# Banded attention on one core: the values become the stationary operand, the result stays feature-major, and w_out's rows are reordered to match

## The chip, the core and the metric

The kernel runs as one program on one core of a Trainium2 chip. The core has a matrix engine (TensorE, written PE in the profile), a vector engine (DVE), a scalar engine (ACT), a general engine (POOL) and a queue processor (SP) that issues nearly all of the transfers. The metric is the device time of one execution in microseconds (us). Three runs of the kernel before gave 2034.96, 2035.17 and 2035.97 us; the median is 2035.17 us.

## The reference, cut to what matters

One layer of a decoder is computed for a prompt of 1024 tokens and for a sample group of 8 sequences with 8 new tokens each. All arithmetic is in float32.

```python
x = x + 0.5 * rms_norm(swiglu(rms_norm(x, norm_ffn1_pre), ...), norm_ffn1_post)
z = rms_norm(x, norm_mix_pre) @ w_in + b_in     # q, k, v and the four HGRN2 parts
# attention, 8 query heads on 2 key/value heads, window 128, one learned sink per head
s = einsum('bnqhgd,bnkhd->bnhgqk', q, k) * SCALE          # 128 queries by 256 keys, banded
p = exp(s - m) / (sum(exp(s - m)) + exp(sink - m))
a = einsum('bnhgqk,bnkhd->bnqhgd', p, v)                  # 512 features per token
a = rms_norm(a, attn_out_norm)                            # over the 512 features
# HGRN2: o, S = hgrn2_chunked(...), for the sample group from eight stored states
x = x + rms_norm(concat([a, o]) @ w_out, norm_mix_post)
x = x + 0.5 * rms_norm(swiglu(rms_norm(x, norm_ffn2_pre), ...), norm_ffn2_post)
```

The order in which the 512 attention features are held is free, as long as the rows of `w_out` and the gains `attn_out_norm` are held in the same order.

## The kernel before

The 1088 tokens are cut into three tiles, n = 0, 1, 2. Tile 0 has 320 tokens: two prompt blocks of 128 and the 64 sample tokens. Tiles 1 and 2 have three prompt blocks each. The two feed-forward layers (`make_ffn`) and the projections `w_in` and `w_out` make up most of the work. Each of their products is made of three float32r matmuls on two halves of each operand (`mm3`, L273 to L275), so that a weight tile is loaded by a transfer into one of three `raw` buffers, rounded on ACT (`split`, L252) and its remainder taken on DVE (L253).

The mixing (attention and HGRN2) runs as a stream of small steps beside these long matmuls. `mixer(n)` chains the attention blocks (`attn_block`) and, step by step in turn with them, the HGRN2 blocks (`hgrn_block`); each `yield` ends a step. `tick()` stands between the pieces of the long matmuls and lets each stream go forward by its rate; `need()` runs the rest of a stream at once. The program is then put through a scheduler (`schedule_with_timeline_sim=True`), which sets the final order of the instructions on each engine from its own model of their times. At run time every engine goes through its list strictly in that order.

An attention block has 128 queries. It is worked off in two passes (`pr`), each with two heads of each of the two key/value groups g. A pass has these steps: four score products (`sc`, L1099), whose operands lie in partitions 0 to 63 for g = 0 and 64 to 127 for g = 1; mask and maximum on DVE (L1107); the exponential on ACT (L1116); eight transposes of the probabilities on PE (`pT`, L1127) and their copy to SBUF on DVE (L1130); and the products with the values (`pv`, L1140). In the kernel before, the transposed probabilities (128 keys by 128 queries) are the stationary operand and 64 columns of the values move, once per head and key block: eight matmuls in a pass. The result has queries in partitions. After both passes DVE divides by the denominators (L1147), `finish_attn` takes the sum of squares on ACT (L1068), the inverse root on DVE in eight small operations (`rsqrt`), scales (L1071), transposes the four 128-wide parts back on PE (`oT`, L1075), applies the gains (L1077), and `put_mix` (L1062, L1063) writes the two halves into `MT`, the stationary or moving operand of the `w_out` products.

All small products are plain float32. The trace writes two matmuls and two weight loads for each such instruction, and one of each for a transpose. All of them share four PSUM banks (the tag `ax`); the long matmuls have four of their own (`mm`).

For the sample tokens, `sample_attn` has four rounds of products with cached and new values: L1326 (128 cached keys) and L1329 (8 new keys) in turn for four sequences, each sequence with 32 result partitions of its own. `sample_hgrn` has for each of four heads one product of L1365 (all 64 tokens) and eight of L1368, one per stored state: a stationary tile of 64 columns, in which the tokens of the other sequences are masked to zero (L1360, on POOL), against 128 moving columns.

`w_out` is loaded by one transfer per weight tile, eight tiles for each n.

## Time and profile before

| what | value |
|---|---|
| median of three runs | 2035.17 us |
| time of the profiled execution | 2035.28 us |
| span from its first to its last instruction | 2033.6 us |
| PE busy | 2002.3 us, 98% |
| DVE busy | 1445.4 us, 71% |
| ACT busy | 921.4 us, 45% |
| POOL busy | 550.4 us, 27% |
| the mixing steps | from 743 to about 1375 us |

A row of a group names the line, engine and operation, then out<-in by the program's names, the shapes, and xcount; behind the bar stand the busy time of the group in us, the mean length of one in ns, and the idle time of the engine just before them with what ended it. A shape such as `128*64 128x256` on PE means 128 rows by 64 columns of stationary operand and 256 moving columns. Matmuls overlap, so that the mean length of one is larger than its share of the time: the busy time of a group divided by its count is nearer to what it costs. In a timeline, a row has its start, its length until the last end, the line, the operation and the count of equal instructions merged; the distance of two starts is what the first one costs.

### The profile page before, as it was taken

Reading aid. Unit: us, or ns where it says so; the run is one execution under the profiler, and the core shown is the slowest. Engines: PE = TensorE matmul, PEld = TensorE weight load, DVE = VectorE, ACT = ScalarE, POOL = GpSimd, SP = SyncE. Lnnn points to the kernel's source line nnn. Section 1 sums busy time; section 2 is a strip of 40 time slices with the busy share of each in tenths; the row PEclk is TensorE's granted clock in tenths of the full one; section 3 lists DMA queues with packets and bytes.
Section 4 is the critical chain, followed back from the end, with each engine's and each line's share of the span. In section 5 each row is a group of like instructions: output and inputs, shape, how many; then the busy total and the mean of one; then the engine's idle time right before and its main releaser. Section 6 shows DMA issues by size and latency. Waiting matters only on the chain.

```text
span 2033.6 us, 34788 instructions
## 1 busy us (share of the span) xinstructions
PE 2002.3 (98%) x13337; PEld 1870.8 (92%) x13337; DVE 1445.4 (71%) x2429; ACT 921.4 (45%) x1647; POOL 550.4 (27%) x508
## 2 busy tenths in 40 slices
PE   9999999999999999899999999999999999999998
PEld 8999999999998988698899897998999999999886
DVE  5776667886568557877668856766889888655667
ACT  6534333444445435435343443644544444445452
POOL 0013333654104101311213311210146555510201
PEclk9999999999999999899999999999999999999999
DMA  8455445656777545546434243526565556576874
GB/s 253 143 158 164 146 143 164 205 179 217 234 240 215 169 147 180 166 127 182 133 96 146 83 142 94 172 95 208 158 203 195 199 175 202 207 236 223 287 258 136
DMA packets 371975, 360.09 MB, mean 177 GB/s; under 512 B 40194, under 2 KB 293969, under 8 KB 371793
## 3 DMA queue, kind: packets, MB, share of 16 engines
q1 hardware_dynamic: 371009, 356.42, 55.2%
q8 instruction: 105, 1.72, 0.4%
q10 hardware_dynamic: 800, 1.44, 0.2%
q14 instruction: 61, 0.50, 0.1%
HBM read 279.85 MB, written 78.94 MB: 176 GB/s over the span
## 4 chain that ended last, share of the span: by engine, by line
PE 94%; DVE 3%; DMA 2%; issue 1%; ACT 0%; DVEq 0%; SPq 0%; ACTq 0%
PE mm L273 27%; PE mm L274 27%; PE mm L275 27%; PE pv L1140 1%; PE c L275 1%; PE c L273 1%; PE c L274 1%; DMA raw<-in_ffn_w_gu_dram 1%; PE sc L1099 1%; PE lv L1171 1%; PE pT L1127 1%; PE tr L492 1%; DMA xt<-x1N 0%; PE l L1195 0%; PE sav L1368 0%
## 5 line engine op out<-in xcount | busy, mean ns | idle before, releaser
L273 PE MATMUL mm<-h,wsph 128*128 128x320 f32 (+1 forms) x1296 | 413.5, 321 | 3.5 <-DVE big L1451 3.1
L274 PE MATMUL mm<-h,wsph 128*128 128x320 f32 (+1 forms) x1296 | 412.1, 318 | 0.0
L275 PE MATMUL mm<-h,wspl 128*128 128x320 f32 (+1 forms) x1296 | 411.0, 318 | 0.0
L252 ACT CAST wsph<-raw 128x1024 fp32r<-128x1024 f32 x202 | 211.4, 1048 | 300.2 <-PE mm L274 240.2
L253 DVE TENSOR_TENSOR wspl<-raw,wsph 128x1024 fp32r<-128x1024 f32 x202 | 251.8, 1249 | 112.4 <-ACT wsph L252 112.0
L253 DVE TENSOR_TENSOR w<-raw,w 128x512 fp32r<-128x512 f32 (+1 forms) x226 | 248.0, 1101 | 92.1 <-ACT w L252 90.3
L252 ACT CAST w<-raw 128x512 fp32r<-128x512 f32 (+1 forms) x226 | 169.5, 754 | 209.8 <-PE mm L274 112.8
L273 PEld LDWEIGHTS mm<-h,wsph 128*128 128x128 f32 x1296 | 244.7, 189 | 8.3 <-DVE big L1451 3.5
L274 PEld LDWEIGHTS mm<-h,wsph 128*128 128x128 f32 x1296 | 245.1, 189 | 2.3 <-issue 1.0
L275 PEld LDWEIGHTS mm<-h,wspl 128*128 128x128 f32 x1296 | 244.7, 189 | 2.4 <-issue 1.8
L273 PE MATMUL mm<-h,w 128*128 128x384 f32 x704 | 235.6, 335 | 0.8 <-DVE big L720 0.8
L274 PE MATMUL mm<-h,w 128*128 128x384 f32 x704 | 235.6, 335 | 0.0
L275 PE MATMUL mm<-h,w 128*128 128x384 f32 x704 | 230.3, 335 | 0.0
L274 PE MATMUL mm<-w,h 128*128 128x512 f32 x462 | 181.0, 392 | 0.0
L273 PE MATMUL mm<-w,h 128*128 128x512 f32 x462 | 180.2, 393 | 0.0
L275 PE MATMUL mm<-w,h 128*128 128x512 f32 x462 | 179.7, 392 | 0.0
L275 PE MATMUL mm<-big,w 128*128 128x384 f32 x528 | 176.6, 335 | 1.2 <-DVE w L253 1.2
L704 POOL TENSOR_TENSOR big<-big 128x384 f32<-128x384 f32 x88 | 111.8, 1271 | 240.1 <-ACT big L717 121.2
L273 PE MATMUL mm<-big,w 128*128 128x384 f32 x528 | 176.6, 334 | 0.0
L274 PE MATMUL mm<-big,w 128*128 128x384 f32 x528 | 176.5, 334 | 0.0
L253 DVE TENSOR_TENSOR w<-t,w 128x512 fp32r<-128x512 f32 x176 | 161.0, 924 | 17.5 <-ACT w L252 17.3
L273 PEld LDWEIGHTS mm<-h,w 128*128 128x128 f32 x704 | 132.1, 188 | 1.3 <-DVE big L720 1.2
(349 smaller groups left out, 3874.1 us busy)
## 6 DMA issues: line engine op xcount, KB each, us to landing
raw<-in_ffn_w_gu_dram SPq DMA_DIRECT2D x156, 512.0 KB
raw<-in_ffn_w_down_dram SPq DMA_DIRECT2D x74, 512.0 KB
raw<-in_w_in_dram SPq DMA_DIRECT2D x54, 512.0 KB
ar<-fa SPq DMA_DIRECT2D x70, 384.0 KB
big<-in_ffn_w_down_dram SPq DMA_DIRECT2D x88, 256.0 KB
fb<-big SPq DMA_DIRECT2D x44, 512.0 KB
raw<-fb SPq DMA_DIRECT2D x40, 512.0 KB
fa<-big SPq DMA_DIRECT2D x22, 768.0 KB
```

The source lines that it names most:

```text
L252: S.copy(hi, src)
L253: (lo_eng or V).tensor_tensor(lo, src, hi.bitcast(F32), op=ALU.subtract)
L273: PE.matmul(out, a[0], b[0], start=first, stop=False, skip_group_check=resume)
L274: PE.matmul(out, a[0], b[1], start=False, stop=False, skip_group_check=resume)
L275: PE.matmul(out, a[1], b[0], start=False, stop=last, skip_group_check=resume)
L492: PE.transpose(bank[:, i * P:(i + 1) * P], y[kh][:, i, k * P:(k + 1) * P], ident)
L704: G.tensor_tensor(e[:, i], e[:, i], e[:, i + 1], op=ALU.mult)
L1099: PE.matmul(banks[g][:, i * 256:i * 256 + wk], zq[64 * g:64 * g + 64, 2 * pr + i, b * P:(b + 1) * P], kx[64 * g:64 * g + 64, k0:k0 + wk], ...
L1127: PE.transpose(bank[:, (i * nk + kb) * P:(i * nk + kb + 1) * P], pt[g][:, i, kb * P:(kb + 1) * P], ident)
L1140: PE.matmul(ob[:, hd * 64:hd * 64 + 64], pT[g][:, (i * nk + kb) * P:(i * nk + kb + 1) * P], vn[:, vb, g * 64:g * 64 + 64], start=kb == 0, ...
L1171: PE.matmul(b4[cs, a, :32], x[:, a, cs], y[:, a, cs], start=True, stop=True)
```

## The change

In `attn_block` the probabilities are divided by their denominator before they are transposed: DVE adds the sink's part and takes the reciprocal in each pass, then DVE scales the two heads of g = 0 and ACT the two of g = 1. The products with the values have the values as the stationary operand (128 keys by 64 features) and the transposed probabilities of two heads as 256 moving columns. The group g = 0 writes result partitions 0 to 63 and g = 1 partitions 64 to 127, in turn, so the result of a block has features in partitions: chunk m holds head m in its lower half and head 4 + m in its upper half. A pass has four such matmuls (two in the first block, which has one key block).

`finish_attn_t` takes the place of `finish_attn` for the prompt blocks. ACT squares the result from PSUM, PE sums over the features with four matmuls whose moving operand is one column of ones (`ms`, L1094), DVE takes the inverse root and puts it on a diagonal (L1098), one matmul with a stationary tile of ones spreads it over all partitions (L1100), ACT copies that to SBUF (L1102), and DVE multiplies result, gains and inverse root in four pieces (L1105). The transposes `oT` of the prompt blocks are gone; the sample tokens still go through `finish_attn`.

The gains and the rows of `w_out` are loaded in the new order: a `w_out` tile of the attention half comes with two transfers of 64 partitions, and for n = 0, where a tile holds both halves, with three instead of one. The sample products are split into 32-column pieces that alternate over result partitions.

```diff
             for pr in range(2):
...
+                V.tensor_tensor(of(mx[:, 2], pr), of(mx[:, 1], pr), of(sm[:, 2], pr), op=ALU.add)
+                V.reciprocal(of(mx[:, 3], pr), of(mx[:, 2], pr))
+                for g in range(2):
+                    for i in range(2):
+                        hd = 4 * g + 2 * pr + i
+                        t, r_ = pt[g][:, i, :wk], mx[:, 3, hd:hd + 1]
+                        if g:
+                            S.activation(t, t, AF.Copy, scale=r_)
+                        else:
+                            V.tensor_scalar(t, t, r_, None, op0=ALU.mult)
                 yield
...
-                for g in range(2):
-                    for i in range(2):
-                        hd = 4 * g + 2 * pr + i
-                        for kb in range(nk):
-                            vb = b + kb + (1 if first else 0)
-                            PE.matmul(ob[:, hd * 64:hd * 64 + 64],
-                                      pT[g][:, (i * nk + kb) * P:(i * nk + kb + 1) * P],
-                                      vn[:, vb, g * 64:g * 64 + 64], start=kb == 0, stop=kb == nk - 1)
-                yield
-            V.tensor_tensor(mx[:, 2], mx[:, 1], sm[:, 2], op=ALU.add)
-            V.reciprocal(mx[:, 3], mx[:, 2])
-            o = t2()
-            V.tensor_tensor(o.rearrange("p (h d) -> p h d", h=8), ob.rearrange("p (h d) -> p h d", h=8),
-                            mx[:, 3].unsqueeze(2).to_broadcast([P, 8, 64]), op=ALU.mult)
-            yield from finish_attn(n, o, P, slice(b * P, (b + 1) * P))
+                for kb in range(nk):
+                    vb = b + kb + (1 if first else 0)
+                    for g in range(2):
+                        PE.matmul(ob[64 * g:64 * g + 64, pr * 256:pr * 256 + 256],
+                                  vn[:, vb, g * 64:g * 64 + 64],
+                                  pT[g][:, :2 * wk].rearrange("p (i k t) -> p k i t", i=2, k=nk)[:, kb],
+                                  start=kb == 0, stop=kb == nk - 1, skip_group_check=True)
+                if pr == 0:
+                    yield
+            yield from finish_attn_t(n, ob, slice(b * P, (b + 1) * P))
...
+        def finish_attn_t(n, ob, sl):
+
+            sm, sq = small(), t2()
+            S.activation(sq, ob, AF.Square)
+            yield
+            bank = axbank("ms")
+            for m in range(4):
+                PE.matmul(bank[:, P:P + 1], sq[:, m * P:(m + 1) * P], ones[:, 0:1], start=m == 0, stop=m == 3)
+            V.tensor_scalar(sm[:, 0, 0:1], bank[:, P:P + 1], 1.0 / 512, EPS, op0=ALU.mult, op1=ALU.add)
+            rsqrt(sm[:, 1, 0:1], sm[:, 0, 0:1], (sm[:, 2, 0:1], sm[:, 3, 0:1]))
+            dg = sq[:, :P]
+            V.tensor_scalar(dg, ident, sm[:, 1, 0:1], None, op0=ALU.mult)
+            yield
+            PE.matmul(bank[:, :P], ones, dg, start=True, stop=True)
+            rb = sq[:, P:2 * P]
+            S.copy(rb, bank[:, :P])
+            o = t2((P, 4, P))
+            for m in range(4):
+                V.scalar_tensor_tensor(o[:, m], ob[:, m * P:(m + 1) * P], cols[:, C_AON + m:C_AON + m + 1], rb,
+                                       op0=ALU.mult, op1=ALU.mult)
+            put_mix(n, 0, sl, o)
+            yield
...
                     for i in range(4):
                         PE.matmul(ob[32 * i:32 * i + 32, :64], pT[:, 0, 32 * i:32 * i + 32],
-                                  vc[:, i, g * 64:g * 64 + 64], start=True, stop=False)
+                                  vc[:, i, g * 64:g * 64 + 64], start=True, stop=False, skip_group_check=True)
+                    for i in range(4):
                         c = i * P + g * 64
                         PE.matmul(ob[32 * i:32 * i + 32, :64], pT[:8, 1, 32 * i:32 * i + 32],
-                                  vnb[hb][:8, c:c + 64], start=False, stop=True)
+                                  vnb[hb][:8, c:c + 64], start=False, stop=True, skip_group_check=True)
...
-                PE.matmul(ob[:r, a * P:(a + 1) * P], At[:r, a, :r], z["v"][:r, 2, a * P:(a + 1) * P],
-                          start=True, stop=False)
-                for b in range(8):
-                    PE.matmul(ob[:r, a * P:(a + 1) * P], qm[:, b], st[:, b], start=False, stop=b == 7)
+                sr = [slice(32 * hf, 32 * hf + 32) for hf in range(2)]
+                for hf in range(2):
+                    PE.matmul(ob[sr[hf], a * P:(a + 1) * P], At[:r, a, sr[hf]], z["v"][:r, 2, a * P:(a + 1) * P],
+                              start=True, stop=False, skip_group_check=True)
+                for b in range(4):
+                    for hf in range(2):
+                        PE.matmul(ob[sr[hf], a * P:(a + 1) * P], qm[:, hf, b], st[:, 4 * hf + b], start=False,
+                                  stop=b == 3, skip_group_check=True)
...
+        def w_out_rows(k0, k1, c0, c1):
+
+            if k0 >= 4:
+                return [((ALL, slice(k0, k1) if c1 - c0 == P else ALL), w_out[k0 * P:k1 * P, c0:c1].rearrange(
+                    "(k p) m -> p k m", p=P))]
+            return [((slice(64 * g, 64 * g + 64), slice(k0, k1) if c1 - c0 == P else ALL),
+                     w_out[256 * g + 64 * k0:256 * g + 64 * k1, c0:c1].rearrange("(k p) m -> p k m", p=64))
+                    for g in range(2)]
...
-                    wt = load_up(w_out, d * P)
+                    wt = load_w(w_out_rows(0, 4, d * P, d * P + P) + w_out_rows(4, 8, d * P, d * P + P), pp, "wsp", 8)
```

The scheduler sets the order anew, so the change also moves instructions that the diff doesn't touch. Three places on PE show it; in their rows the size is that of the result (partitions by columns), the numbers tell buffers apart, and the line numbers are those of each kernel (L278 to L280 after are L273 to L275 before, L1204 is L1171, L1165 is L1127, L1228 is L1195, L1277 is L1244 and L454 is L449).

The first is the end of the second attention block of tile 0, around 847 us. `lv` and `l` are levels of HGRN2, `tr` and `kT` are transposes of other streams. Before:

```order
L275 MATMUL mm_8255<-w_8375,h_8433 128x512
L1171 MATMUL lv_8285<-t_1112_7909,t_1113_7910 32x32 x16
L1140 MATMUL pv_8007<-vn_6437,t_1159_8243 128x64 x4
L1140 MATMUL pv_8007<-vn_6437,t_1161_8250 128x64 x4
L1195 MATMUL l_1178_8352<-t_1112_7909,t_1113_7910 32x32 x8
L1195 MATMUL l_1186_8418<-t_1112_7909,t_1113_7910 64x64 x4
L1075 MATMUL oT_8456<-ident,t_1184_8404 128x128 x4
L449 MATMUL tr_8469<-ident,big_5758 128x128 x3
L449 MATMUL tr_8475<-ident,big_5758 128x128 x3
L1244 MATMUL kT_8481<-ident,t_1113_7910 128x128 x4
L449 MATMUL tr_8488<-ident,big_5758 128x128 x3
L273 MATMUL mm_8650<-h_8465,wsph_8646 128x384
```

After:

```order
L280 MATMUL mm_8274<-w_8393,h_8450 128x512
L1204 MATMUL lv_8217<-t_1112_7926,t_1113_7927 32x32 x16
L1165 MATMUL pT_8257<-ident,t_1139_8106 128x128 x4
L1165 MATMUL pT_8264<-ident,t_1140_8109 128x128 x4
L1204 MATMUL lv_8304<-t_1112_7926,t_1113_7927 32x32 x16
L1176 MATMUL pv_8024<-t_1159_8262,vn_6438 64x256
L1176 MATMUL pv_8024<-t_1161_8269,vn_6438 64x256
L1176 MATMUL pv_8024<-t_1159_8262,vn_6438 64x256
L1176 MATMUL pv_8024<-t_1161_8269,vn_6438 64x256
L1228 MATMUL l_1180_8370<-t_1112_7926,t_1113_7927 32x32 x8
L1094 MATMUL ms_8420<-ones,t_1173_8333 128x1 x4
L1228 MATMUL l_1187_8435<-t_1112_7926,t_1113_7927 64x64 x4
```

The wait for the transposes `oT` has left the list there (the spreading product comes 21 rows behind `ms`), but the transposes `pT` and one more `lv` now stand in the same run without a long matmul between them; before, eleven long matmuls stood between those and the rest.

The second is a pass of the second block of tile 1, where the products with the values stand among long matmuls. Before:

```order
L274 MATMUL mm_11100<-h_9245,wsph_11096 128x384
L1171 MATMUL lv_11028<-t_1537_10662,t_1538_10663 32x32 x16
L1140 MATMUL pv_10777<-vn_8641,t_1583_11000 128x64 x4
L1140 MATMUL pv_10777<-vn_8641,t_1585_11007 128x64 x4
L275 MATMUL mm_11100<-h_9243,wspl_11097 128x384
```

After:

```order
L278 MATMUL mm_11222<-h_9261,wsph_11218 128x384
L1176 MATMUL pv_10826<-t_1583_11051,vn_8658 64x256
L279 MATMUL mm_11222<-h_9263,wsph_11218 128x384
L1176 MATMUL pv_10826<-t_1585_11058,vn_8658 64x256
L1176 MATMUL pv_10826<-t_1583_11051,vn_8658 64x256
L1176 MATMUL pv_10826<-t_1585_11058,vn_8658 64x256
L280 MATMUL mm_11222<-h_9261,wspl_11219 128x384
```

The first product of g = 0 stands alone, and a long matmul separates it from the other three. Of the 16 passes, five have all four products in one run, two (the first block) have their two in one run, and nine are cut into one and three like this one.

The third is a round of the sample attention. Before:

```order
L1326 MATMUL spv_8717<-kv_8583,t_1233_8666 32x64
L1329 MATMUL spv_8717<-vnew_8525,t_1233_8666 32x64
L1326 MATMUL spv_8717<-kv_8583,t_1233_8666 32x64
L1329 MATMUL spv_8717<-vnew_8525,t_1233_8666 32x64
L1326 MATMUL spv_8717<-kv_8583,t_1233_8666 32x64
L1329 MATMUL spv_8717<-vnew_8525,t_1233_8666 32x64
L1326 MATMUL spv_8717<-kv_8583,t_1233_8666 32x64
L1329 MATMUL spv_8717<-vnew_8525,t_1233_8666 32x64
```

After:

```order
L1259 MATMUL hT_8699<-ident,t_1225_8639 128x128 x4
L1359 MATMUL spv_8734<-kv_8600,t_1233_8683 32x64 x4
L1363 MATMUL spv_8734<-vnew_8542,t_1233_8683 32x64 x4
L1204 MATMUL ld_8771<-big_6780,big_6644 32x32 x8
L1334 MATMUL ssc_8803<-big_8546,t_1213_8564 32x136 x4
```

The four products with cached values now follow each other, and so do the four with new values, each set over four different groups of 32 result partitions.

34 lines of the change are left out of this document (18 added, 16 removed).

## The prediction

> **What bounds the kernel now.** I read the page's shares and chain first, then two stretches of the mixing.
>
> ```profile
> span 2033.6 us, 34788 instructions
> PE 2002.3 (98%) x13337; PEld 1870.8 (92%) x13337; DVE 1445.4 (71%) x2429; ACT 921.4 (45%) x1647; POOL 550.4 (27%) x508
> PE 94%; DVE 3%; DMA 2%; issue 1%; ACT 0%; DVEq 0%; SPq 0%; ACTq 0%
> ```
>
> ```profile
> 743.00:1375.00 632.00, 618.30 (x5245) 545.48 (x5245) 452.61 (x1083) 287.32 (x591) 128.06 (x182) 0.99 0.46 136
> 843.00:865.00 22.00, 13.31 (x149) 11.73 (x150) 19.67 (x54) 12.35 (x28) 6.32 (x8) 0.77 0.64 163
> ```
>
> PE is busy for 98% of the span and is 94% of the chain. In the mixing it is idle for 632.0 - 618.3 = 13.7 us, of which 22.0 - 13.31 = 8.7 us lie between 843 and 865, where DVE is busy for 19.67 of 22 us. So the time of the change is PE's time for the altered products, plus what it does to waits, chiefly in that stretch. The sum is made against the profiled execution, 2035.28 us (1.7 around the span); the median of the runs, 2035.17, is 0.1 lower. The next rows are PE's groups.
>
> ```profile
> L1140 PE MATMUL pv<-vn,t 128*128 128x64 f32 x240 | 29.8, 274 | 0.1
> L1127 PE MATMUL pT<-ident,t 128*128 128x128 f32 x120 | 16.9, 277 | 0.0
> L1075 PE MATMUL oT<-ident,t 128*128 128x128 f32 x32 | 5.3, 292 | 3.5 <-DVE t L1071 3.5
> L1171 PE MATMUL lv<-t,t 128*32 128x32 f32 x1328 | 19.9, 199 | 2.4 <-DVE sm L1144 1.2 <-DVE sm L390 0.7 <-DVE t L1206 0.2
> L1195 PE MATMUL l<-t,t 128*32 128x32 f32 x128 | 4.7, 198 | 0.9 <-DVE t L1206 0.9
> L324 PE MATMUL st<-omean,ss 128*128 128x1 f32 x20 | 2.5, 229 | 0.0
> L336 PE MATMUL rb<-dg,ones 128*128 128x320 f32 x10 | 3.6, 442 | 0.0
> ```
>
> Of two equal shapes, `lv` goes round four column strips and costs 19.9/1328 = 15 ns a record; `l` stays in one strip and costs 4.7/128 = 37 ns. So column strips do overlap here, by a factor of 2.5 over four. For wider products the timeline of PE shows single runs among long matmuls, from several places:
>
> ```profile
> 1014.92 0.31 PE L275 MATMUL mm<-h,wspl 128*128 128x320 f32 x1
> 1015.07 1.89 PE L1140 MATMUL pv<-vn,t 128*128 128x64 f32 x16
> ...
> 1017.00 0.31 PE L274 MATMUL mm<-h,wsph 128*128 128x320 f32 x1
> 1017.15 0.31 PE L275 MATMUL mm<-h,wspl 128*128 128x320 f32 x1
> ...
> 1020.80 0.31 PE L275 MATMUL mm<-h,wspl 128*128 128x320 f32 x1
> 1021.04 1.14 PE L1099 MATMUL sc<-kx,big 64*128 64x256 f32 x8
> 1022.11 0.41 PE L273 MATMUL mm<-h,wsph 128*128 128x320 f32 x1
> 1022.36 0.31 PE L274 MATMUL mm<-h,wsph 128*128 128x320 f32 x1
> ...
> 1053.41 0.34 PE L275 MATMUL mm<-h,wspl 128*128 128x384 f32 x1
> 1053.68 1.13 PE L1099 MATMUL sc<-kx,big 64*128 64x256 f32 x4
> ...
> 1055.02 0.34 PE L274 MATMUL mm<-h,wsph 128*128 128x384 f32 x1
> 1055.20 0.34 PE L275 MATMUL mm<-h,wspl 128*128 128x384 f32 x1
> ```
>
> I call the cost of a run the distance from the long matmul before it to the second one behind it, less two ordinary steps (0.15 us each at 320 columns, 0.18 at 384). `pv`, 16 records: 1017.00 - 1014.92 - 0.29 = 1.79, or 0.112 a record. `sc` going between the two groups, 8 records: 1.56 - 0.29 = 1.27. `sc` of one group alone, 4 records: 1.61 - 0.35 = 1.26. Eight records in two strips cost what four cost in one: two strips overlap fully, at 1.07/4 = 0.267 us a record and strip, and entering and leaving such a run costs about 0.2 together (0.24 and 0.25 where an ordinary step is 0.15).
>
> **The change, part by part.**
>
> *Products with the values.* Before: 240 records at 0.112 = 26.9 us. After, 60 instructions, 120 records of 256 moving columns. One record costs at most `sc`'s 0.267, and half of its weight columns are gone; a full load is about 0.11 (`pv`'s record is no shorter), so half a load saves up to 0.055: 0.21 to 0.267, I take 0.24. The order decides how many overlap: five passes in one run, 4 x 0.24 + 0.2 = 1.16 each; nine cut, where the lone product costs 2 x 0.24 + 0.2 = 0.68 and the other three again 1.16 (two of the three share a strip); two short ones of the first block, 0.68 each. That is 5.8 + 16.6 + 1.4 = 23.8: 3.1 us less. Bounds: with 0.21 and no loss from the cuts 15.8 (-11); with no overlap at all 120 x 0.267 + 25 x 0.2 = 37 (+10). Only the Trainium skill speaks against the strips: "TensorE: Matmul & The Clock Gate", Part 3, says that a weight load overlaps matmuls in flight only if its row group differs. Column strips share their rows, so by that rule each of the 120 loads (about 53 ns, an estimate from the page's load formula for 64 columns) would stand in line, and the sum would be some 3 us higher. The 15 ns of `lv`, less than the 27 ns that the same formula gives for its load alone, disagree with it; I don't count it.
>
> *End of a block.* Added on PE for eight blocks: `ms`, 64 records with a full load and one column, 0.112 (load, as `pv`) to 0.125 (`st`, 2.5/20): 7.2 to 8.0; `L1100`, 16 records, by `rb` 0.36 x 128/320 = 0.144: 2.3. Removed: 32 transposes, 0.112 (a full load) to 0.165 (their row): 3.6 to 5.3. Net +4.2 to +6.7; I take +5, as the load was the price in `pv`. The DVE rows that go:
>
> ```profile
> L1147 DVE TENSOR_TENSOR t<-pv,sm 128x512 f32<-128x512 f32 x8 | 5.5, 684 | 4.0 <-PE pv L1140 4.0
> L1071 DVE TENSOR_SCALAR t<-t,sm 128x512 f32<-128x512 f32 x8 | 4.2, 526 | 0.2
> L1077 DVE TENSOR_TENSOR t<-oT,cols 128x512 f32<-128x512 f32 x8 | 5.5, 689 | 3.5 <-PE oT L1075 3.2
> L1116 ACT ACTIVATE t<-t,sm 128x256 f32<-128x256 f32 (+1 forms) x64 | 30.9, 485 | 37.9 <-DVE sm L1112 30.5 <-DVE sm L1118 7.4
> ```
>
> That is 1.9 us a block on DVE; it gets four scalings of 256 columns (half of L1071's, 1.1 us), four multiplications of 128 (a quarter of L1077's or a bit more, 0.7 to 1.4), a diagonal and four small ones: about as much, up to +1.5 a block, under PE in a stage where DVE is busy for 72%. ACT gets four scalings as long as its exponentials, 2 us a block, and is busy for 45%. Both cost nothing while PE has long matmuls.
>
> *Scores.* Their products stay, but the order puts them into two runs of one group in eight of the 16 passes where it was seven: 2 x 1.26 - 1.27 = +1.25, from 0 to +2.5; I take +1.
>
> *Sample products.* The run of HGRN2's stored states and a round of the attention products:
>
> ```profile
> 953.24 0.30 PE L1326 MATMUL spv<-kv,t 128*32 128x64 f32 x2
> ...
> 955.05 0.87 PE L449 MATMUL tr<-ident,big 128*128 128x128 f32 x6
> ...
> 983.85 0.44 PE L273 MATMUL mm<-h,wsph 128*128 128x384 f32 x1
> 984.23 1.96 PE L1368 MATMUL sav<-big,t 128*64 128x128 f32 x16
> ...
> 986.40 0.34 PE L275 MATMUL mm<-h,wspl 128*128 128x384 f32 x1
> ```
>
> `sav` costs 2.55 - 0.35 = 2.20 for 16 records, 0.125 each without 0.2. In two strips by turns: 8 x 0.125 + 0.2 = 1.2, a gain of 1.0 for each of four heads, less 0.2 for each of three cuts: -3.4 (0 without overlap, -4.5 without cuts). L1365's product becomes two halves side by side: nothing. The POOL mask of half the size hides under PE. `spv` costs 955.05 - 953.24 = 1.81 and 0.2 a round. After: 16 records of twice `l`'s moving width, 2 x 37/2.5 = 30 ns, 0.5 us, and 0.3 for two sets; 1.2 us less in each of four rounds: -4.8 (-3 to -6).
>
> *Transfers.* 16 more issues for n = 0 and 8 for n = 1 and 2, none with more bytes. SP needs 0.37 us for one, and no wait of PE in the mixing names a transfer; the weights are asked for well ahead. Nothing, +3 if a split load lands late. The extra transfer of gains lies in the first feed-forward stage: nothing.
>
> ```profile
> 971.79 0.37 SPq L259 DMA_DIRECT2D raw<-in_w_out_dram  x1
> ```
>
> *Waits.* The long gap of PE:
>
> ```profile
> 846.87 0.39 PE L275 MATMUL mm<-w,h 128*128 128x512 f32 x1
> ...
> 855.23 1.08 PE L1195 MATMUL l<-t,t 128*64 128x64 f32 x8 [3.22 <-DVE t L1206]
> ...
> 859.78 1.09 PE L1075 MATMUL oT<-ident,t 128*128 128x128 f32 x4 [3.46 <-DVE t L1071]
> ...
> 863.26 0.42 PE L273 MATMUL mm<-h,wsph 128*128 128x384 f32 x1
> ```
>
> For 16 us PE does only small pieces, and DVE's list sets the pace. The 3.46 us before `oT` go, for the spreading product stands 21 rows later; what is late next is the transposes `tr` and the rounded tiles behind them, which wait for the same DVE list, now with the scaling at its head. I take -2, from -6 to +4. Elsewhere the transposes `pT` now wait for one more step: two small DVE operations, two scalings of 0.26 on DVE and two of 0.49 on ACT beside them, about 1.3 us; behind them on both engines stand the weight roundings. Before, `pT` never waited (its row: 0.0), so most of it hides; +0.5, at worst 16 x 1.3 = +21.
>
> Sum: -3.1 + 5 + 1 - 3.4 - 4.8 - 1.5 = -6.8, so 2035.28 - 6.8 = 2028.5 us.
>
> **Rivals.**
> *The strips do better.* For it: `sc` overlaps fully; against it: nine cut passes. Values at -8 instead of -3.1, the gap at -5 instead of -2: 2021, and 2016 at the ends of both.
> *The longer way to the transposes takes the gain back.* For it: ACT's scaling queues behind roundings, and several passes have few long matmuls between scores and transposes. Against it: the idle 0.0. At 0.3 to 0.6 us a pass it costs 5 to 10: 2033 to 2038, no change. From 0.7 us a pass, 2040 and slower.
> *Wide column streams don't overlap.* Only 32-wide ones are seen to, and `sc`'s strips are strips of rows. Then values cost +10 and `sav` gains nothing: 13 + 3.4 more than forecast, 2045. It decides once a record in two strips costs over 0.21 us instead of 0.12, which makes up the 11 us to the upper edge of no change. Against it: `lv`.
>
> **How the numbers follow.** What a measurement tells from no change is about 0.2%, 4 us. Forecast (2023 to 2031): 0.46. Strips better: 0.18. Gain taken back to within 4 us: 0.21. Slower by the longer way: 0.08; by streams that don't overlap: 0.07. So faster 0.64, same 0.21, slower 0.15. From 2016 to 2040 all but the slower cases and the far end of the first rival are in.
>
> **What would show it.** `pv` at 0.12 us a record in whole runs and 0.24 where it stands alone; `ms` near 0.11; `sav` and `spv` at half their busy time; `oT` only four records; PE's idle time in the mixing no longer than 14 us; idle before `pT` near 0. The prediction is wrong if `pv` keeps over 0.2 us a record in its whole runs, or if `pT`, `ms` or L1100 show waits of over 5 us together.

## The result and the profile after

Six runs of the changed kernel took 2045.63 to 2051.17 us, median 2049.18; the six runs of the kernel before beside them have a median of 2035.07. The ratio is 1.0066, with a 95% interval of 1.0053 to 1.0079: the change costs 14 us where a gain of 7 was forecast. The profiled execution took 2047.08 us, 11.8 more than that of before. First the page of the changed kernel, span and busy time.

```profile
span 2045.3 us, 34828 instructions
PE 2006.7 (98%) x13273; PEld 1856.7 (91%) x13273; DVE 1452.6 (71%) x2493; ACT 933.5 (46%) x1679; POOL 550.1 (27%) x508
```

Span less PE's busy time is 38.6 us, before it was 31.3: idle time has grown although PE's list has 64 records fewer. PE is also busy for 4.4 us more.

Both traces have 10294 records of long matmuls, so the same record can be looked up in each. The 4300th starts 0.3 us earlier after than before, the 6800th 11.3 us later, and at the end it is 11.7. The whole loss lies in the mixing. The windows below run from the 4300th to the 6900th long matmul (stretch; then PE, weight loads, DVE, ACT, POOL; then the granted clock of TensorE), and under each stand the parts of it in which the trace has the granted clock at half. Before:

```profile
738.35:1412.14 673.79, 657.06 (x5469) 577.60 (x5468) 477.76 (x1136) 305.29 (x626) 128.06 (x182) 0.99 0.46 138
852.99:863.23 10.24, 4.53 (x25) 4.41 (x26) 8.16 (x22) 3.02 (x8) 2.08 (x4) 0.50 0.42 102
1266.01:1272.83 6.82, 6.04 (x23) 6.04 (x24) 5.18 (x27) 2.17 (x9) 0.00 (x0) 0.50 0.12 35
```

After:

```profile
738.02:1423.41 685.39, 663.30 (x5405) 565.01 (x5404) 484.24 (x1200) 317.44 (x658) 129.58 (x182) 0.97 0.46 136
847.40:867.88 20.48, 14.52 (x97) 10.88 (x98) 15.89 (x47) 9.61 (x22) 4.42 (x8) 0.50 0.52 136
1239.94:1243.34 3.40, 3.14 (x7) 2.49 (x8) 2.69 (x8) 3.07 (x13) 0.80 (x2) 0.50 0.00 0
1267.24:1274.06 6.82, 5.33 (x16) 4.42 (x17) 6.41 (x29) 2.63 (x14) 0.00 (x0) 0.50 0.28 83
1355.99:1362.81 6.82, 6.05 (x51) 4.57 (x52) 4.69 (x10) 3.38 (x5) 0.66 (x1) 0.50 0.39 103
```

The stretch is 11.6 us longer. PE is idle for 685.39 - 663.30 = 22.1 us in it, before for 16.7: +5.4. At half clock it works for 14.52 + 3.14 + 5.33 + 6.05 = 29.0 us, before for 10.6; if work at half clock takes twice as long, 14.5 us are lost, before 5.3: +9.2. What is left, length less idle less that loss, is PE's own work at full clock: 685.4 - 22.1 - 14.5 = 648.8, before 651.8: -3.0. So the work did get less, and waits and clock took back nearly five times as much. Set against the sum of the prediction, PE's work is 2.3 us above its forecast (-3.0 for -5.3), the waits are 6.9 above theirs (+5.4 for -1.5), and 9.2 belong by this reckoning to the clock, for which the sum has no term.

By place, between the same long matmuls, the changed kernel gains 2.7 us up to the 5100th (974 us: the crowd of small pieces near 850 us and the sample products, which alone gain 7.8 there), loses 1.8 from there to the 6200th (1230 us), and loses 12.5 from there to the 6900th, in the mixing of tile 2. Of these 12.5 us, 6.0 are idle time, 4.2 the loss at half clock and 2.2 work.

The two longest waits of PE after, by who ended them:

```profile
PE pT L1165 <- DVE t L1158: 4.4, 2, 2.5
PE mm L278 <- DVE big L1496: 2.6, 3, 1.5
```

At the head stands the wait of the transposes for the scaled probabilities (L1158), which did not exist before. 1.9 us of it lie near 848 us, 2.5 us in the last block. PE in the last block, from the scores to the next long matmuls:

```profile
1346.91 1.14 PE L1127 MATMUL sc<-kx,big 64*128 64x256 f32 x8
...
1353.77 0.46 PE L1204 MATMUL lv<-t,t 128*32 128x32 f32 x32 [0.68 <-DVE sm L1146]
1356.76 1.54 PE L1165 MATMUL pT<-ident,t 128*128 128x128 f32 x6 [2.53 <-DVE t L1158]
1358.23 0.66 PE L1204 MATMUL lv<-t,t 128*32 128x32 f32 x32
...
1361.19 0.47 PE L280 MATMUL mm<-h,wspl 128*128 128x320 f32 x1
1361.45 0.47 PE L278 MATMUL mm<-h,wsph 128*128 128x320 f32 x1
```

After the waits of 0.68 and 2.53 us, long matmuls that take 0.147 us a step elsewhere take 0.26 (1361.19 to 1361.45), until the clock is back at 1362.8. What PE waited for stands on ACT and DVE:

```profile
1355.71 0.19 ACT L1147 ACTIVATE sm<-sm 128x4 f32<-128x4 f32 x1
1355.81 1.03 ACT L255 CAST wsph<-raw 128x1024 fp32r<-128x1024 f32 x1
1356.74 0.91 ACT L1156 ACTIVATE t<-t,sm 128x256 f32<-128x256 f32 x2
```

```profile
1355.94 0.17 DVE L1149 TENSOR_TENSOR sm<-sm,sm 128x4 f32<-128x4 f32 x1 [0.52 <-ACT sm L1147]
1356.13 0.18 DVE L1150 RECIPROCAL sm<-sm 128x4 f32<-128x4 f32 x1
1356.35 0.62 DVE L1158 TENSOR_SCALAR t<-t,sm 128x256 f32<-128x256 f32 x2
```

From the end of the last exponential (1355.90) to the scaled tile of g = 0 (1356.97) it is 1.1 us; g = 1 stands behind a weight rounding of 1.03 us on ACT and comes at 1357.65. The scaling also has to wait for all four exponentials and for the sink's, because the denominators of all four heads are added in one operation (L1149), while the transposes of g = 0 need only the first two exponentials, which end at 1354.73. So the new step keeps PE from these transposes for 2.0 us, until 1356.76.

Near 848 us the way is much longer, though the operations are the same:

```profile
840.00 0.19 ACT L1147 ACTIVATE sm<-sm 128x4 f32<-128x4 f32 x1
```

```profile
842.40 0.75 DVE L426 SCALAR_TENSOR_TENSOR big<-big,sm,xt 128x512 f32<-128x512 f32 x1 [4.35 <-DMA xt<-in_x_prompt_dram]
...
846.06 0.15 DVE L1149 TENSOR_TENSOR sm<-sm,sm 128x4 f32<-128x4 f32 x1
846.91 1.20 DVE L426 SCALAR_TENSOR_TENSOR big<-big,sm,xt 128x512 f32<-128x512 f32 x1 [0.69 <-DMA xt<-in_x_prompt_dram]
...
848.24 0.62 DVE L1158 TENSOR_SCALAR t<-t,sm 128x256 f32<-128x256 f32 x2
```

The last exponential ends at 840.2 us and the scaled tile comes at 848.85, 8.7 us later: on DVE's list the four operations stand between additions of the residual (L426), which wait for transfers of `xt`. In eight of the sixteen passes this way takes 1.06 or 1.07 us, in seven 0.9 to 3.6. Before, DVE waited for `xt` there too, 4.24 us, but the transposes did not depend on it.

Before, the pass of the last block had its transposes 7.5 us behind its scores with no wait:

```profile
1339.86 1.13 PE L1099 MATMUL sc<-kx,big 64*128 64x256 f32 x4
...
1347.36 1.09 PE L1127 MATMUL pT<-ident,t 128*128 128x128 f32 x8
```

In its order 36 long matmuls stand between the two; after, 29 do, for a longer way. This count alone does not tell which passes wait: in the changed kernel the pass near 1128 us has 26 and does not wait, and the one near 848 us has 42 and waits 1.9 us. The groups of PE that changed:

```profile
L1176 PE MATMUL pv<-t,vn 128*64 128x256 f32 x120 | 24.8, 418 | 1.1 <-DVE t L1168 1.1
L1094 PE MATMUL ms<-ones,t 128*128 128x1 f32 x64 | 8.5, 254 | 0.0
L1406 PE MATMUL sav<-big,t 128*32 128x128 f32 x64 | 5.3, 277 | 0.0
L1100 PE MATMUL ms<-t,ones 128*128 128x128 f32 x16 | 3.4, 293 | 0.0
L1359 PE MATMUL spv<-kv,t 128*32 128x64 f32 x32 | 1.3, 231 | 0.0
L1363 PE MATMUL spv<-vnew,t 8*32 8x64 f32 x32 | 1.3, 226 | 0.0
```

`pv` has 24.8 us instead of 29.8, `sav` 5.3 instead of 8.3, the two `spv` groups together 2.25 instead of 7.53 (before, their rows overlap in time, so that the busy times of the two groups, 4.8 and 4.7, must not be added); `oT` keeps 4 of its 36 records.

### The profile page after: what moved, and what is told of

Its sections match the earlier page's. It is cut to its first block, busy times and chain, and to the rows that moved or that the text cites. A ratio compares the mean times of both kernels' runs of the same rounds, so it can differ in the third digit from the quotient of the medians.

```text
span 2045.3 us, 34828 instructions
## 1 busy us (share of the span) xinstructions
PE 2006.7 (98%) x13273; PEld 1856.7 (91%) x13273; DVE 1452.6 (71%) x2493; ACT 933.5 (46%) x1679; POOL 550.1 (27%) x508
## 4 chain that ended last, share of the span: by engine, by line
PE 91%; DVE 3%; DMA 3%; ACT 1%; issue 1%; SPq 0%; DVEq 0%; ACTq 0%
PE mm L278 27%; PE mm L279 26%; PE mm L280 26%; PE c L280 1%; PE c L278 1%; PE c L279 1%; PE sc L1127 1%; DMA ar<-fa 1%; PE pv L1176 1%; DMA raw<-in_ffn_w_gu_dram 1%; PE lv L1204 1%; PE pT L1165 1%; PE tr L497 1%; DVE w L256 1%; DMA xt<-in_x_prompt_dram 0%
## 5 line engine op out<-in xcount | busy, mean ns | idle before, releaser
L278 PE MATMUL mm<-h,wsph 128*128 128x320 f32 (+1 forms) x1296 | 414.7, 322 | 3.7 <-ACT sg L632 2.2
L280 PE MATMUL mm<-h,wspl 128*128 128x320 f32 (+1 forms) x1296 | 411.7, 318 | 0.0
L278 PEld LDWEIGHTS mm<-h,wsph 128*128 128x128 f32 x1296 | 244.6, 189 | 11.0 <-issue 3.1
L280 PEld LDWEIGHTS mm<-h,wspl 128*128 128x128 f32 x1296 | 244.7, 189 | 4.0 <-issue 3.5
L278 PE MATMUL mm<-h,w 128*128 128x384 f32 x704 | 235.8, 335 | 1.2 <-DVE big L725 1.2
L280 PE MATMUL mm<-h,w 128*128 128x384 f32 x704 | 230.5, 335 | 0.0
L278 PE MATMUL mm<-w,h 128*128 128x512 f32 x462 | 180.8, 395 | 0.5 <-DVE big L905 0.5
L280 PE MATMUL mm<-w,h 128*128 128x512 f32 x462 | 179.5, 392 | 0.0
L280 PE MATMUL mm<-big,w 128*128 128x384 f32 x528 | 176.8, 335 | 1.5 <-DVE w L256 1.5
L278 PE MATMUL mm<-big,w 128*128 128x384 f32 x528 | 176.6, 335 | 0.0
L278 PEld LDWEIGHTS mm<-h,w 128*128 128x128 f32 x704 | 132.2, 188 | 1.6 <-DVE big L725 1.6
```

Of the source, the lines that this page charges most:

```text
L278: PE.matmul(out, a[0], b[0], start=first, stop=False, skip_group_check=resume)
L280: PE.matmul(out, a[1], b[0], start=False, stop=last, skip_group_check=resume)
```

## The experiments

The theory: the loss is the longer way to the transposes, which shows where few long matmuls cover it, and the half clock behind such waits; the sample products gain what was forecast. The rivals are named with each run. All medians below stand beside the kernel before on the same chip (2034.8 to 2036.0 us). The table has the stretch from the 4300th to the 6900th long matmul in the profiled execution of each, taken apart as above. The ratio is the one on record; it is not the quotient of two medians of the table.

| kernel | median, us | ratio to before, 95% interval | idle | at half clock | own work |
|---|---|---|---|---|---|
| before | 2035.1 | | 16.7 | 10.6 | 651.8 |
| changed | 2049.2 | 1.0066, 1.0053 to 1.0079 | 22.1 | 29.0 | 648.8 |
| sample products alone | 2027.0 | 0.9947, 0.9932 to 0.9962 | 16.2 | 10.1 | 642.2 |
| attention alone | 2047.5 | 1.0048, 1.0031 to 1.0065 | 19.2 | 30.1 | 653.9 |
| changed, no scaling | 2037.6 | 1.0004, 0.9995 to 1.0014 | 18.5 | 23.3 | 646.5 |
| changed, g = 1 first | 2041.4 | 1.0024, 1.0014 to 1.0034 | 22.5 | 24.2 | 643.0 |
| changed, idle work | 2046.1 | 1.0054, 1.0039 to 1.0069 | 20.8 | 15.8 | 656.6 |
| before, with scaling | 2039.6 | 1.0016, 1.0007 to 1.0025 | 18.9 | 17.0 | 651.2 |
| g = 1 first, rate 1.4 | 2035.8 | 1.0004, 0.9994 to 1.0013 | 23.0 | 24.5 | 639.6 |
| that, rate of tile 0 1.05 | 2043.6 | 1.0038, 1.0025 to 1.0051 | 30.2 | 28.7 | 638.3 |
| changed, rate 1.4 | 2039.0 | 1.0019, 1.0009 to 1.0029 | 21.4 | 19.1 | 645.4 |
| g = 1 first, rate 1.2 | 2040.0 | 1.0020, 1.0011 to 1.0030 | 24.8 | 27.1 | 639.8 |
| sample products, rate 1.4 | 2026.2 | 0.9960, 0.9946 to 0.9975 | 17.8 | 9.7 | 640.9 |

**The two halves of the change.** The first is the kernel before with the sample products of the change:

```diff
-                PE.matmul(ob[:r, a * P:(a + 1) * P], At[:r, a, :r], z["v"][:r, 2, a * P:(a + 1) * P],
-                          start=True, stop=False)
-                for b in range(8):
-                    PE.matmul(ob[:r, a * P:(a + 1) * P], qm[:, b], st[:, b], start=False, stop=b == 7)
+                for b in range(4):
+                    for hf in range(2):
+                        PE.matmul(ob[sr[hf], a * P:(a + 1) * P], qm[:, hf, b], st[:, 4 * hf + b], start=False,
+                                  stop=b == 3, skip_group_check=True)
...
```

> The kernel before with the split sample products alone (stored states and cached values in alternating column groups); attention, w_out and gains as before. Theory (the products got cheaper by what PE's timeline of the changed kernel shows, and the loss sits only in the attention's waits and in the halved clock behind them): rounds of spv cost 1.33 us less, four of them 5.3, and sav's busy time falls by 3.0, so 2035.1 - 8.3 = 2026.8 us (2024 to 2030), with the granted clock at 0.5 in no more stretches than before. Rival (the sample split itself shifts the order so that another wait or cold stretch opens): 2034 or slower.

It took 2027.0 us. Its order behind the sample work hardly changes, and nearly all of the gain arises there: its long matmuls run 0.1 us later than those of before at the 4700th, 8.0 earlier at the 5100th and 8.6 at the 6200th. This version beats both kernels.

The second is the changed kernel with the sample products as before (the same edit, undone).

> The changed kernel with the sample products as before. Theory (attention carries the whole loss): 2049.2 + 8.3 = 2057.5 us (2053 to 2061), with idle of PE and halved clock in the mixing as large as in the changed kernel (22 us idle, about 29 us of work at half clock). Rival (the loss came from both parts meeting in the crowded stretch near 850 us): 2047 or faster.

It took 2047.5 us, at the edge of the rival. So the attention alone costs 12 us, and yet the sample products, which gain 8 to 9 alone, gain nothing measurable on top of it. The long matmuls show where: the changed kernel is ahead of this one by 9.0 us at the 6200th and by 12.4 at the 6600th (1338 us), and by 2.9 at the 6800th. The gain is there and is lost again in the last block, in which this kernel has waits of 1.9 us before `pT` and 0.3 before `pv`, and no half clock. The rival's place was wrong: the stretch near 850 us is as cold here (20.5 us) as in the changed kernel.

**The scaling taken out.**

```diff
-                V.tensor_tensor(of(mx[:, 2], pr), of(mx[:, 1], pr), of(sm[:, 2], pr), op=ALU.add)
-                V.reciprocal(of(mx[:, 3], pr), of(mx[:, 2], pr))
-                for g in range(2):
-                    for i in range(2):
...
-                        if g:
-                            S.activation(t, t, AF.Copy, scale=r_)
-                        else:
-                            V.tensor_scalar(t, t, r_, None, op0=ALU.mult)
```

> The changed kernel without the division of the probabilities: the addition, the reciprocal and the four scalings ahead of the transposes are left out, so the attention is not divided by its denominators. Theory (the longer way from the exponential to the transposes makes PE wait, and the clock halves behind each such wait): the waits before pT go, PE's idle time in the mixing falls from 22 to 17 us or less, work at half clock from 29 to about 11 us, together 14 us: 2049.2 - 14 = 2035 us (2031 to 2039). Rival (the waits come from the new end of a block, ms and its inverse root, and from the order as a whole): 2044 to 2049 and the cold stretch near 850 us as long as now (20 us).

It took 2037.6 us, 11.6 less, inside the theory's range. But only a part is waits: idle falls by 3.6 us and the loss at half clock by 2.9. Its order has five cut passes of `pv` where the changed kernel has nine, and PE's own work is 2.2 us less. The stretch at half clock near 850 us stays at 17.1 us, which the theory did not expect: the scaling is not what makes that one long.

In one pass of this kernel PE waits for the exponentials themselves. The transposes start behind the first of them, which ends at 1236.79, while the others run until 1238.28:

```profile
1236.28 0.51 ACT L1144 ACTIVATE t<-t,sm 128x256 f32<-128x256 f32 x1 [3.23 <-DVE sm L1140]
...
1238.27 0.19 ACT L1147 ACTIVATE sm<-sm 128x4 f32<-128x4 f32 x1
```

```profile
1236.94 0.44 PE L1155 MATMUL pT<-ident,t 128*128 128x128 f32 x2 [0.47 <-ACT t L1144]
```

With the scaling no transpose can start before 1238.46, when the sink's exponential ends, and the scaling itself comes on top.

**The cut runs of the values.**

```diff
-                    for g in range(2):
+                    for g in (1, 0):
                         PE.matmul(ob[64 * g:64 * g + 64, pr * 256:pr * 256 + 256],
```

> The changed kernel with the products of the values in the order g = 1, g = 0 instead of g = 0, g = 1, nothing else. In the static order all 16 passes then have their four products in one run, where nine were cut into one and three. Theory (a cut run pays its entry twice): a run of two records costs 0.79 us and one of six 1.21, a whole run of eight 1.22, so nine joined runs save 9 x 0.78 = 7.0 us: 2042 us (2039 to 2045), if the waits stay as they are. Rival (the first product now waits for the copy that lands last, and the chain behind it gets longer): no gain, 2049 or slower, with idle before pv of over 3 us.

It took 2041.4 us, 7.8 less than the changed kernel, for 7.0 expected; PE's own work is 5.8 us less, and the wait before `pv` grew from 1.1 to 2.2 us only. A cut pass of the changed kernel and a whole one here:

```profile
1032.47 0.31 PE L280 MATMUL mm<-h,wspl 128*128 128x320 f32 x1
1032.71 0.65 PE L1176 MATMUL pv<-t,vn 128*64 128x256 f32 x2
...
1033.57 0.34 PE L279 MATMUL mm<-h,wsph 128*128 128x384 f32 x1
...
1034.44 0.34 PE L278 MATMUL mm<-h,wsph 128*128 128x384 f32 x1
1034.71 1.08 PE L1176 MATMUL pv<-t,vn 128*64 128x256 f32 x6
...
1035.99 0.34 PE L280 MATMUL mm<-h,wspl 128*128 128x384 f32 x1
```

```profile
1011.38 0.31 PE L280 MATMUL mm<-h,wspl 128*128 128x320 f32 x1
1011.62 1.08 PE L1176 MATMUL pv<-t,vn 128*64 128x256 f32 x8
...
1012.89 0.31 PE L279 MATMUL mm<-h,wsph 128*128 128x320 f32 x1
```

Less two ordinary steps, the cut pass costs 1.10 - 0.32 = 0.78 and 1.55 - 0.35 = 1.20, the whole one 1.51 - 0.29 = 1.22. The product that stands alone is nearly pure loss: of the other three, two are of the same strip, so that the three take as long as all four.

**Idle work in the gaps.** Nothing is left out; the throwaway products are overwritten by the real ones.

```diff
+                    if g == 0 and (n, b, pr) in ((0, 1, 1), (2, 2, 1)):
+                        for _ in range(6):
+                            PE.matmul(bank[:8, :256], ident[:, :8], amask, start=True, stop=True)
...
+                if (n, b, pr) in ((0, 1, 1), (2, 2, 1)):
+                    for _ in range(3):
+                        PE.matmul(ob[:64, pr * 256:pr * 256 + 256], vn[:, b, :64], pT[0][:, :256], start=True,
+                                  stop=True, skip_group_check=True)
```

> The changed kernel with idle work for PE ahead of the two worst passes (second block of tile 0, last block of tile 2): six throwaway products ahead of the transposes pT and three ahead of the products with the values, in places where PE waits; their results are overwritten, the order of the rest of PE is nearly the same. Theory (the clock halves because PE does too little for some microseconds, so work in the gaps keeps it up): the wait of 2.5 us near 1354 stays as time but is filled, the stretch at half clock behind it (6.8 us, 6.06 us of work) goes, 3.0 us less; near 850 the half-clock stretch shrinks from six steps of 3.41 us to four or fewer, 3.4 us less: 2043 us (2039 to 2046). Rival (the clock falls whatever PE does there, or the throwaway work costs its own time): 2049 to 2053, with the stretches as long as now.

It took 2046.1 us, just past the upper edge of the range. The clock does what the theory says at both places. The last block has no half clock any more:

```profile
1340.00:1366.00 26.00, 23.76 (x291) 17.36 (x290) 16.59 (x37) 14.12 (x24) 5.91 (x10) 1.00 0.32 95
```

Near 850 us, 10.2 us at half clock are left of 20.5, and the eight transposes there, of the changed kernel and of this one, show what the clock does to the same work:

```profile
848.65 1.97 PE L1165 MATMUL pT<-ident,t 128*128 128x128 f32 x8 [1.90 <-DVE t L1158]
```

```profile
849.75 1.09 PE L1168 MATMUL pT<-ident,t 128*128 128x128 f32 x8
```

But the time hardly follows. The throwaway work costs more than the gaps it fills (own work +7.8 us), and near 850 the next waits grow: `lv` from 1.7 to 2.0 us, `pv` from 1.1 to 3.1. DVE sets the pace there, so PE at full clock waits longer. A part of the loss that the table books to the clock in that stretch is therefore no loss of time; how large a part can't be told from these runs.

**The scaling on the old order.** The scaling of the changed kernel goes into each pass of the kernel before, and the multiplication at the end of a block becomes a copy:

```diff
             o = t2()
-            V.tensor_tensor(o.rearrange("p (h d) -> p h d", h=8), ob.rearrange("p (h d) -> p h d", h=8),
-                            mx[:, 3].unsqueeze(2).to_broadcast([P, 8, 64]), op=ALU.mult)
+            V.tensor_copy(o, ob)
```

> The kernel before with the division moved ahead of the transposes in each pass (the addition, the reciprocal, two scalings on DVE and two on ACT, as in the changed kernel); the multiplication at the end of a block becomes a plain copy. Products with the values, end of a block, sample products as before. Theory (the longer way to the transposes costs by itself): between the changed kernel and the one without the scaling PE's idle time in the mixing differs by 22.1 - 18.5 = 3.6 us and the loss at half clock by 14.5 - 11.7 = 2.8, so 2035.1 + 6.4 = 2041.5 us (2038 to 2046). Rival (the order before has enough long matmuls between scores and transposes to hide it, 36 in the last pass where the changed kernel has 29): 2033 to 2037, idle before pT under 1 us.

It took 2039.6 us (interval 1.0007 to 1.0025): +3.5, between the rival and the theory's middle. No wait before `pT` came up in the last block; but in this order 46 long matmuls stand there between scores and transposes, not the 36 of the kernel before, so the rival's point was not put to the test. The loss is in the crowd near 850 us, where the scaling again stands on DVE among additions that wait for `xt` (4.73 and 0.33 us):

```profile
PE oT L1075 <- DVE t L1071: 5.2, 1, 5.2
...
PE pT L1137 <- DVE t L1130: 2.1, 1, 2.1
```

**Cover instead of a shorter way.** `RM[2]` is the rate at which the mixing of tile 2 goes forward between long matmuls; the first of three runs has the changed kernel with this one number altered.

```diff
-    RM = [0.95, 1.0, 1.3]
+    RM = [0.95, 1.0, 1.4]
```

> The changed kernel with one number different: the rate of tile 2's mixing steps, 1.3 to 1.4; the division and the order of the products stay as changed. The last pass then has 46 long matmuls between its scores and its transposes instead of 29. Theory (the loss near 1340 to 1363 us comes from too little cover for the longer way): its waits, 1.3 + 0.7 + 2.5 us, and the half clock behind them, 6.06/2 = 3.0, go, 7.5 us together; as in the run with g = 1 first at the same rate, one wait of 2.6 us before pT near 1295 may come up instead: 2049.2 - 7.5 + 2.6 = 2044 us (2040 to 2046). Rival (the longer way costs wherever the pass stands): 2049 or slower, with the same idle and half clock in the mixing.

It took 2039.0 us, 10.2 less, and better than expected: two passes fewer are cut (2 x 0.78 = 1.6), and the stretch at half clock near 1241 us is gone. Idle time falls by only 0.7 us, because a wait of 2.0 us before `pT` came up near 1300 us, in a pass with 38 long matmuls, as had been feared. The last pass now has its transposes 9.7 us behind its scores and waits for nothing:

```profile
1338.00:1364.00 26.00, 25.01 (x344) 22.14 (x343) 18.33 (x47) 13.56 (x23) 5.66 (x7) 1.00 0.39 111
```

```profile
1338.91 1.13 PE L1127 MATMUL sc<-kx,big 64*128 64x256 f32 x8
...
1348.60 0.60 PE L1165 MATMUL pT<-ident,t 128*128 128x128 f32 x4
```

With `g` = 1 first as well:

> The changed kernel with g = 1 first (2041.4 us) and one number more: the rate at which the steps of tile 2's mixing go forward between long matmuls, 1.3 to 1.4. In the static order the last pass then has 46 long matmuls between its scores and its transposes (26 at 1.3, 29 in the changed kernel, 36 in the kernel before). Theory (that cover decides whether the way to the transposes shows): the waits of the last pass, 2.1 + 0.95 us, and the half clock behind them, 3.3/2 = 1.7, go: 2041.4 - 4.7 = 2036.7 us (2034 to 2039). Rival (the chain of DVE and ACT is too slow in any case, so that the wait moves to other passes): 2041 or slower.

It took 2035.8 us, level with the kernel before (0.9994 to 1.0013). A wait of 2.6 us before `pT` came up near 1297 us, again in a pass with 38 long matmuls, so the rival holds in part: the longer way shows somewhere at any rate that was tried. The other direction:

> The changed kernel with g = 1 first and the rate of tile 2's mixing at 1.2 instead of 1.3. In the static order the last five passes then have 36, 59, 39, 55 and 48 long matmuls between scores and transposes. Theory (cover of 36 or more hides the longer way): no wait before pT behind 1280 us and no half clock there, against 2041.4 us at rate 1.3 the 3.1 us of waits and 1.7 of half clock are gone: 2036.6 us or less; against rate 1.4 (2035.8 us) the waits near 1295 and 1354, 3.0 and 1.0 us, and 1.7 of half clock: down to 2031 (2030 to 2037). Rival (steps left over at the end of tile 2 are then run at once, without long matmuls between them): 2041 or slower.

It took 2040.0 us, between the two. The waits before `pT` near 1297 and 1350 us are gone, but a pass that stands in a row of small pieces near 1281 us has waits before and behind its transposes (1.1, 0.9, 0.7 and 1.5 us in turn, with 10.2 us at half clock). It is the pass with 59 long matmuls between scores and transposes, so the theory that 36 or more hide the longer way is wrong: its scaled tile came 11.8 us after its scores.

And the rate of tile 0, on top of `g` = 1 first and 1.4:

> As the run before, and the rate of tile 0's mixing from 0.95 to 1.05. In the static order the transposes of the fourth pass (pT, near 850 us) then stand ahead of twelve long matmuls and no longer in the crowd of small pieces, as in the kernel before; but more small pieces of the sample tokens stand behind it in the crowd. Theory (the transposes in the crowd, each waiting for DVE, make the long stretch at half clock): it falls from 17 us of the clock's time to 10, 12.6/2 - 4.5/2 = 4 us less than the run before: 2032.7 us (2030 to 2036). Rival (any crowd of small pieces on DVE's list keeps the clock down, and the longer one does so for longer): 2038 or slower.

It took 2043.6 us. The rival's number came, for another reason than either gave: the sample tokens' steps now come before their cached keys have landed.

```profile
PE pT L1165 <- DVE t L1158: 6.2, 2, 3.6
PE skT L1321 <- DMA kv<-in_cache_k_win_dram: 5.2, 2, 2.7
```

The control has the sample products alone at rate 1.4:

> A control for the change of rate: the kernel before with the split sample products alone (2027.0 us) and the rate of tile 2's mixing at 1.4 instead of 1.3, attention as before. Theory (the rate only helps where the longer way to the transposes waits; here no pass waits before pT): nothing to gain, 2027 us (2025 to 2030). Rival (1.4 is a better rate for any of these kernels, and the gain of 10 us in the changed kernel is no sign of the longer way): 2020 or faster.

It took 2026.2 us, no different from 2027.0 within the spread of its runs (2024.4 to 2028.1). So the rate by itself gains nothing where no pass waits before `pT`.

## Why the prediction was wrong

**Values: right way, too large.** Forecast -3.1. A whole run costs 1.22 us (1.16 forecast), a cut one 0.78 + 1.21 = 1.99 (0.68 + 1.16 = 1.84), one of the first block 0.79: 5 x 1.22 + 9 x 1.99 + 2 x 0.79 = 25.6 us against 26.9 by the same reading before, -1.3. (The busy time of the group falls by 5.0, but it leaves out the entry and exit of each run, which lie in the steps beside it.) The number of cuts was read rightly from the order; a lone strip costs 0.29 us a record, not 0.24. Column strips do overlap, so that rival fell. The half-price load that the 0.24 counted on did not show: a record that stands alone costs as much as the upper price, `sc`'s 0.267, or more. Uncut, the values would have gained 14 x (1.79 - 1.22) + 0.2 = 8.2.

**End of a block: right.** Forecast +5. Where they stand among long matmuls, `ms` costs 0.90 us a block and L1100 0.22, and the transposes had cost 0.44: 8 x (0.90 + 0.22 - 0.44) = +5.4.

**Sample products: right.** Forecast -8.2; the run with them alone gained 8.7 by its median, and PE's own work 9.6. Each round of `spv` gained 1.3 us where 1.2 were forecast.

**Scores and transfers: nothing against them.** The order has 24 runs of `sc` after and 22 before, and the group is busy for 26.4 us instead of 24.0, part of it at half clock: the +1 was not told apart. Behind the mixing the distance between the two kernels stays within 0.7 us to the end, and no wait of PE there names a transfer of weights. The split transfers were not tried alone.

**Waits: this step failed.** The prediction put "-1.5" for them, -2 in the crowd and +0.5 for the longer way, "at worst +21". Idle time in the mixing grew by 5.4 us. In the crowd it did shrink, from 9.5 us to 8.1 (the five gaps over 0.5 us in each), nearly as forecast. The longer way was undersized. The prediction counted the work of the new operations, 1.3 us beside each other, and that is nearly what they take where nothing stands between them (1.06 us for g = 0). But it left out two things. The step waits for all four exponentials and the sink's, so that the transposes of g = 0 come 2.0 us later in the last block, not 1.1. And its operations take places on the lists of DVE and ACT, and wait there for what stands ahead of them: near 848 us 8.7 us pass from the last exponential to the scaled tile. What was wrong too is the reason that the way would hide, the idle 0.0 before `pT` in the kernel before. That figure says that there was no wait in the old order; it says nothing of how much time was to spare, and the order is a new one. The prediction showed this order for PE alone, at three places, and not for the two engines on which the new step runs.

**And a term was missing.** The clock has no place in the sum, though the row of 843 to 865 us that opens it has 0.77 in the column. In both kernels the clock falls after PE has done little for a few microseconds: in the 3.41 us ahead of the four falls of the changed kernel in the mixing PE was busy for 1.26, 1.46, 1.73 and 0.96 us, ahead of the two of the kernel before for 1.56 and 1.10. By the trace the work at half clock accounts for 9.2 us of the 11.6, the larger part of the loss, with the limit that the fill run showed: where DVE sets the pace, near 850, a slower PE costs less than its share. In the last block there is long work behind the wait, and there it costs in full: 6.05 us of work at half clock, 3.0 us lost. The Trainium skill has the mechanism in "TensorE: Matmul & The Clock Gate", Part 1: the clock is either full or half, and falls after an idle window of about 3.4 us. This case's trace agrees as to the steps: the stretches at half clock last 3.4, 6.8, 10.2 and 20.5 us, 1, 2, 3 and 6 times 3.41. But the windows ahead of the falls were not idle throughout, as the busy times above show. Two falls do not fit even "little work": in the attention alone (952 us) and in the kernel before with scaling (942 us) the clock fell for one step after 3.41 us in which the trace has PE busy all the time, for the most part with small sample products. Why is open.

**The rivals.** The one that came is "the longer way to the transposes takes the gain back", with a chance of 0.21 and 0.08 for its slower end. It was priced at an even 0.3 to 0.7 us for each of 16 passes. In truth few passes pay, two of them 1.9 and 2.5 us and most nothing, and those that pay do so twice, in the wait and in the clock behind it. The range ended at 2040, where the even price reaches 0.7 us a pass. The prediction named it for ACT's scaling behind roundings and for few long matmuls; near 848 us it was DVE's list that held the scaling up, at whose head the prediction had put it.

**What is open.** Taking out the scaling gives back 11.6 of the 14 us. In the profiled executions the stretch is 8.7 us shorter: 6.5 of waits and clock, and 2.2 of work, in an order in which four passes fewer are cut. It does not give back the long stretch near 850 us, which all versions with the new attention have (17 to 24 us), except the one with throwaway work in it. In the order of the changed kernel the transposes and one more `lv` stand in the crowd, which would explain it; the run that moved them out moved other work in and waited for transfers, so that this is argued and not shown. No run changed the place of the scaling on DVE's list alone, so what that place is worth, apart from the order of PE, is read from the traces and not measured.

## What to carry to other kernels

An idle time of 0.0 before an instruction is no measure of slack. To cost a step that is put into a chain, find its place in the new order at every point where it occurs: what it has to wait for, what stands ahead of it on the lists of the engines that run it, and how much work the waiting engine has meanwhile. Counting the long matmuls in between was not enough here, for a pass with 26 did not wait and one with 59 did. A wait of the bounding engine is to be priced with the clock behind it, if the column of the granted clock shows dips where that engine waits already. A change made of two independent parts is worth running in parts: here one half gains 0.5%, the other loses as much, and together they lose 0.7%: the gain of the good half can vanish in a wait of the other.

## What the runs showed of the hardware

- The granted clock has two values here, 1.0 and 0.5, and in the mixing it stays at half for whole steps of 3.41 us. PE was not idle throughout before it fell: in the changed kernel it was busy for 0.96 to 1.73 us of the 3.41 us ahead of each fall in the mixing. Eight transposes take 1.97 us at half and 1.09 at full clock.
- Throwaway matmuls in a wait of 2.5 us kept the clock at full for the long matmuls behind it (granted clock 1.00 from 1340 to 1366 us), where without them it fell for 6.8 us.
- Two column strips of 64, in turn, overlap: eight records of 256 columns take 1.22 us, six of which four are of one strip 1.20, two of a single strip 0.78. So a product that the order leaves alone costs 0.78 us more than in the whole run.
- A round of 16 small records over four column groups of 32 went from 1.81 us to 0.49 when the products that start an accumulation were put ahead of those that end one; before, the two kinds stood in turn on each column group.
